# Smaller first loads on two queues, PSUM banks placed by hand, and a root per tile at the end of a transformer block kernel

## The chip, the cores and the metric

The kernel runs on one core of one Trainium2 chip. A time is the device time of one execution in microseconds; a kernel's time is the median of its runs. Engines are named as in the profile: PE (TensorE matmul; PEld its weight loads), DVE (VectorE), ACT (ScalarE), POOL (GpSimd), SP (SyncE, which here only issues DMAs). ACTq, POOLq and SPq rows are DMA issues of those engines.

## The reference

One block over 1024 tokens of width 1024 in fp32, with 16 learned tokens put in front:

```python
h = concat([meta_tokens, x])                       # 1040 x 1024
u = rms_norm(h, pre_mix_norm) @ w_in               # 2560 columns: b, c, h_a, glu_val, glu_gate (512 each)
y_a = b * causal_conv3(c * h_a, conv_a_w)
z   = causal_conv31(glu_val * sigmoid(glu_gate), conv_b_w) + conv_b_bias
y_b = silu(layer_norm(z))
h   = h + rms_norm(concat([y_a, y_b]) @ w_out, post_mix_norm)
n   = rms_norm(h, pre_ffn_norm)
h   = h + rms_norm((silu(n @ w_gate) * (n @ w_up)) @ w_down, post_ffn_norm)   # inner width 2816
return h[16:]
```

## The kernel before

Every fp32 operand is kept as a rounded part (`h`, "hi") and the rest (`l`, "lo"), and `mm3` (L106) makes a product of three matmuls: hi x hi (L108), hi x lo (L109), lo x hi (L110). ACT rounds (a cast), DVE or POOL subtracts to get the rest. The whole program is under a manual schedule: each engine runs its instructions in the order in which the code issues them, and a tile's buffer is taken again when its last reader is done.

**Stage 1, input projection (to about 242 us).** 20 units of 128 output columns: `g`, `v` (gate and value of the long convolution, four each), then `c`, `h`, `b` (four each). A unit is 8 tiles of x (k = 0 to 7) times three thirds of 348 or 342 columns (`T3`, `C3`), or two halves for `b`, so 72 or 48 matmuls. While x arrives, a first pass (L251 to 258) runs the units g0 and v0 side by side over k. Its loads, L199 and L172, are issued on SP: the first 256 columns of g0's weights (`cut[0]`), x tile 0, the same part of v0, then the other 768 columns of each (`cut[1]`) around x tile 1, then the remaining x tiles. `round_x`/`rest_x` (L178, L181) split an x tile, `split_first` (L203, L204) a part of the weights. Ahead of it 12 calls of a warm-up matmul on the identity run on PE (L88; 24 matmuls in the trace). Then 18 one-column matmuls (`ss_x`, L263) sum the squares of x, `spread_x` (L281) turns the nine columns of roots into a row `rB` by transposes, and the 18 other units follow in a loop (L503). `AT` (L501) says at which unit and k extra work is issued: `start_g` (which calls `spread_x`) at unit 0, k = 2. The convolution's taps run on DVE beside the matmuls, `gate` (L294) and `value` read a unit's PSUM.

**PSUM.** Eight banks: in stage 1 a pool `aux` of two and a pool `ps1` of two buffers of three banks. In stages 2 and 3 `aux` stays and `ps2` has six banks; from product 4 of stage 3 on both are closed for a pool `psf` of eight (L942). Buffers of a pool are taken in turn.

**Stage 2, output projection (242 to 339 us).** `group` (L756) runs over three or two blocks of 128 tokens, two banks each, eight k steps, of which the last two go block by block; `at` says what is issued ahead of a step. `leave_psum` evicts, `norms` scales and adds the residual, and `turn` (L590) transposes a normalised block: four transposes into one bank (L595), copied by ACT (L597), twice per block.

**Stage 3, gate and up projection (339 to 768 us).** A Strassen scheme: 11 pairs (`Pair`, index j) of seven products (n = 1 to 7), each product for two weights (m = 0, 1) of 4 x 3 matmuls of 128x512. `order` (L836) interleaves the first two pairs; from then on a pair runs 1, 6, 2, 5, 7, 3, 4. `a_side` forms a weight operand (`op`, L627 on ACT and L614 on DVE) two products ahead; `leave` (L694) evicts one product later: after product 1 a copy on ACT (L698, tile U), after product 2 a Silu and a DVE product (L704, L617, tile G). Products 2 and 4 accumulate on the banks of 1 and 7 once those have been read. `split` (L730) writes hi and lo of a finished tile to DRAM (`gdA`, `gdS`). The loop is at L938.

**Stage 4, down projection (768 us to the end).** Again seven products, 11 steps each, for four banks `QX` or `QY`: `load` (L1022, POOL queue) brings the tiles `a` back four steps ahead, `side` (L1043) splits the weights into `db`, and `leave1` to `leave7` evict. `finish3` scales and stores the first 512 rows, `finish4` (L1154) the rest: for each of the four last tiles an addition, a sum of squares on ACT (L990), a product with the gain, then roots (`rsqrt_n`, L119) for two tiles, one and one, and `scale` (L998) of both halves of a row block with their output DMAs (L1003, SP).

## Time and profile before

| what | value |
| --- | --- |
| time, median of 3 runs | 996.87 us (993.75 to 997.32) |
| the profiled execution | 994.89 us, its span 993.1 us |
| mean granted TensorE clock | 0.995 |
| PE busy | 967.6 us (97%) |
| DVE, ACT, POOL busy | 723.3, 398.4, 279.9 us |
| moved by DMA | 156.68 MB, 158 GB/s over the span |

A row of the timeline gives the start in us from the span's start, the length, engine, line of the code, operation, written tile <- read tiles with partitions x elements, and how many like it were merged; a bracket behind it holds the idle time of the engine before it and what ended that. A row of the waits gives the waiting engine, tile and line, for whom it waited, then the total, the number of times and the longest. Ends of matmuls are modelled, so their rows overlap; starts are what to compare.

### The profile page before, as it was taken

Reading aid. Unit: us, or ns where it says so; the run is one execution under the profiler, and the core shown is the slowest. Engines: PE = TensorE matmul, PEld = TensorE weight load, DVE = VectorE, ACT = ScalarE, POOL = GpSimd, SP = SyncE. Lnnn points to the kernel's source line nnn. Section 1 sums busy time; section 2 is a strip of 40 time slices with the busy share of each in tenths; the row PEclk is TensorE's granted clock in tenths of the full one; section 3 lists DMA queues with packets and bytes.
Section 4 is the critical chain, followed back from the end, with each engine's and each line's share of the span. In section 5 each row is a group of like instructions: output and inputs, shape, how many; then the busy total and the mean of one; then the engine's idle time right before and its main releaser. Section 6 shows DMA issues by size and latency. Waiting matters only on the chain.

```text
span 993.1 us, 12601 instructions
## 1 busy us (share of the span) xinstructions
PE 967.6 (97%) x4643; PEld 829.3 (84%) x4643; DVE 723.3 (73%) x997; ACT 398.4 (40%) x650; POOL 279.9 (28%) x239
## 2 busy tenths in 40 slices
PE   9999999999999989989999999999999999999995
PEld 8999999998878778878888888888887788888784
DVE  6599999556464799998897887887885442545666
ACT  7533322345454663345343433443433333322331
POOL 0367846442000000443133132231242411121110
PEclk9999999999999999999999999999999999999998
DMA  7111211113351520445623624524319899766776
GB/s 281 45 41 44 71 36 43 64 43 148 128 191 64 185 70 0 170 183 199 233 106 128 220 105 142 188 112 166 148 64 340 271 356 370 244 187 201 263 227 230
DMA packets 58285, 156.68 MB, mean 158 GB/s; under 512 B 6128, under 2 KB 6512, under 8 KB 58224
## 3 DMA queue, kind: packets, MB, share of 16 engines
q1 hardware_dynamic: 41904, 104.16, 28.9%
q0 software_dynamic: 11088, 40.38, 12.6%
q10 hardware_dynamic: 5232, 11.35, 3.1%
q8 instruction: 36, 0.59, 0.3%
q14 instruction: 25, 0.20, 0.1%
HBM read 107.10 MB, written 48.76 MB: 157 GB/s over the span
## 4 chain that ended last, share of the span: by engine, by line
PE 85%; DVE 8%; issue 2%; ACT 2%; DMA 1%; ACTq 0%; DVEq 0%; POOL 0%; SPq 0%; POOLq 0%
PE x L108 6%; PE x L109 6%; PE x L110 6%; PE y L108 5%; PE y L109 5%; PE y L110 5%; PE qx L109 4%; PE qx L108 4%; PE qx L110 4%; PE po L108 3%; PE po L110 3%; PE po L109 3%; PE qy L109 3%; PE qy L110 3%; PE qy L108 3%
## 5 line engine op out<-in xcount | busy, mean ns | idle before, releaser
L614 DVE TENSOR_TENSOR op<-u,op 128x512 fp32r<-128x512 f32 x154 | 145.8, 980 | 24.5 <-ACT op L627 23.4
L627 ACT CAST op<-u 128x512 fp32r<-128x512 f32 x154 | 92.0, 619 | 136.1 <-DVE u L614 77.3
L614 DVE TENSOR_TENSOR db<-wb,db 128x512 fp32r<-128x512 f32 x77 | 55.3, 720 | 91.0 <-ACT db L1051 90.7
L617 POOL TENSOR_TENSOR C<-C,C 128x512 f32<-128x512 f32 x11 | 17.6, 1598 | 325.2 <-ACT C L726 175.6
L1051 ACT CAST db<-wb 128x512 fp32r<-128x512 f32 x77 | 47.3, 621 | 122.3 <-PE qx L110 59.4
L108 PE MATMUL qx<-db,a 128*128 128x512 f32 x176 | 68.7, 390 | 2.4 <-DMA a<-gdA 2.4
L109 PE MATMUL qx<-db,a 128*128 128x512 f32 x176 | 68.6, 390 | 0.3 <-DVE db L614 0.3
L110 PE MATMUL qx<-db,a 128*128 128x512 f32 x176 | 68.5, 389 | 0.0
L611 DVE TENSOR_TENSOR U<-y,U 128x512 f32<-128x512 f32 x66 | 43.8, 682 | 23.5 <-PE y L110 23.5
L617 POOL TENSOR_TENSOR U<-U,U 128x512 f32<-128x512 f32 x22 | 31.6, 1437 | 89.3 <-ACT U L726 58.3
L108 PE MATMUL qy<-db,a 128*128 128x512 f32 x132 | 51.5, 390 | 0.6 <-ACT db L1051 0.6
L109 PE MATMUL qy<-db,a 128*128 128x512 f32 x132 | 51.5, 390 | 0.3 <-DVE db L614 0.3
L110 PE MATMUL qy<-db,a 128*128 128x512 f32 x132 | 51.4, 389 | 0.0
L1027 POOL DMA_DIRECT2D a<-gdS x44 | 23.2, 529 | 93.0 <-PE qy L110 47.4
L344 DVE SCALAR_TENSOR_TENSOR ac<-g,pr,ac 128x512 f32<-128x512 f32 x56 | 41.9, 748 | 0.0
L344 DVE SCALAR_TENSOR_TENSOR ae<-d,pr,ae 128x512 f32<-128x512 f32 x56 | 41.9, 748 | 0.0
L108 PEld LDWEIGHTS qx<-db,a 128*128 128x128 f32 x176 | 33.0, 188 | 9.9 <-issue 2.8
L614 DVE TENSOR_TENSOR u<-u,u 128x512 f32<-128x512 f32 x44 | 39.0, 905 | 0.8
L109 PEld LDWEIGHTS qx<-db,a 128*128 128x128 f32 x176 | 33.0, 188 | 7.4 <-DVE db L614 0.6
L108 PE MATMUL x<-B21h,op 128*128 128x512 f32 x88 | 35.1, 399 | 3.9 <-ACT U L698 3.9
L110 PEld LDWEIGHTS qx<-db,a 128*128 128x128 f32 x176 | 33.0, 188 | 6.9
L108 PE MATMUL y<-T2h,op 128*128 128x512 f32 x88 | 34.3, 390 | 1.7 <-DVE G L617 1.7
(303 smaller groups left out, 2924.7 us busy)
## 6 DMA issues: line engine op xcount, KB each, us to landing
a<-gdS POOLq DMA_DIRECT2D x44, 512.0 KB, 4.5
a<-gdA POOLq DMA_DIRECT2D x33, 512.0 KB, 5.6
u<-w_gate_u SPq DMA_DIRECT2D x22, 512.0 KB, 4.5
u<-w_up_u SPq DMA_DIRECT2D x22, 512.0 KB, 5.6
gdS<-HI SPq DMA_DIRECT2D x44, 256.0 KB, 2.3
gdA<-HI SPq DMA_DIRECT2D x33, 256.0 KB, 2.0
gdS<-GS SPq DMA_DIRECT2D x33, 256.0 KB, 2.7
ws_o<-w_out_u SPq DMA_DIRECT2D x14, 512.0 KB, 5.1
```

The source lines that it names most:

```text
L108: nc.tensor.matmul(o, lh, rh, start=start, stop=False, skip_group_check=again)
L109: nc.tensor.matmul(o, lh, rl, start=False, stop=False, skip_group_check=again)
L110: nc.tensor.matmul(o, ll, rh, start=False, stop=stop, skip_group_check=again)
L344: nc.vector.scalar_tensor_tensor(out if i == n - 1 else acc, src[:, i : i + HALF], w(i), init if i == first else acc, op0=ALU.mult, op1=AL ...
L611: (eng or nc.vector).tensor_tensor(o, a, b, op=ALU.add)
L614: (eng or nc.vector).tensor_tensor(o, a, b, op=ALU.subtract)
L617: (eng or nc.vector).tensor_tensor(o, a, b, op=ALU.mult)
L627: nc.scalar.copy(t[:, 0, :], src)
L1027: nc.gpsimd.dma_start(loads[n, j], gd[an][j])
L1051: nc.scalar.copy(t[:, 0, :], b)
```

## The change

- Six calls of the warm-up instead of twelve.
- First loads: x tile 0 in thirds of its columns; weights in parts of 128, 256 and 640 columns (one, two and five k tiles), the first parts of g0 and v0 on ACT's queue, the rest on SP's. The activation table is loaded behind ACT's two issues.
- The first third of the columns of unit g1 (24 of its 72 matmuls) goes into the first pass, into one bank of `aux`; its unit in the loop keeps two thirds. `gate(1)` reads the two places with one more DVE operation.
- The transposes of `spread_x` are issued in three places (unit 0, k = 2, 4, 6), in the bank of `ss_x`.
- From stage 2 on there are eight pools of one bank. The output projection's blocks take the banks (2, 7), (3, 4), (5, 6), the turns (0, 1), (5, 6) or (2, 7), and the products a list `free`: each takes the first two and gives them back after its eviction.
- Turns are issued one step earlier and one at a time; at product 2 of the order, product 1 is evicted before the turns and not behind them; at product 15 the eviction comes before the splits.
- The first three loads of `a` for stage 4 are issued at the last product of stage 3.
- In stage 4 the product with the gain is issued behind the additions of the same step; at the end each tile has a root of its own, with that product inside it, and its two halves are scaled apart, the second in the wait of the next tile.

The diff, cut:

```diff
-    for i in range(12):
+    for i in range(6):
         nc.tensor.matmul(pw[:, :P], ident, ident, start=True, stop=True)
...
-    def rsqrt_n(ss, inv_n, e, n, name):
+    def rsqrt_n(ss, inv_n, e, n, name, middle=None):
...
         nc.vector.tensor_scalar(v, ss, inv_n, e, op0=ALU.mult, op1=ALU.add)
+        if middle:
+            middle()
...
-    cut = [slice(0, 2 * P), slice(2 * P, D)]
+    cut = [slice(0, P), slice(P, 3 * P), slice(3 * P, D)]
+    FIRST = [("g", 0), ("v", 0), ("g", 1)]
...
-    for j in range(2):
-        load_first("g", cut[j])
-        xs[j] = load_x(j)
-        load_first("v", cut[j])
-    for k in range(2, 5):
+    xs[0] = load_x(0, [third(0)])
+    load_first(FIRST[0], cut[0], nc.scalar)
+    load_first(FIRST[1], cut[0], nc.scalar)
+    table(AF.Abs_reciprocal_sqrt)
+    load_first(FIRST[2], cut[0])
+    for j in (1, 2):
+        nc.sync.dma_start(xs[0][:, third(j)], xT[0][:, third(j)])
+    xs[1] = load_x(1)
+    for u in FIRST:
+        load_first(u, cut[1])
+    xs[2] = load_x(2)
+    for u in FIRST:
+        load_first(u, cut[2])
+    for k in range(3, 5):
         xs[k] = load_x(k)
...
+    split_first(FIRST[0], cut[0])
+    round_x(0, third(0))
+    rest_x(0, third(0))
+    for u in FIRST[1:]:
+        split_first(u, cut[0])
+    for j in (1, 2):
+        round_x(0, third(j))
+        rest_x(0, third(j))
     round_x(1)
     rest_x(1)
-    split_first("v", cut[1])
+    for u in FIRST:
+        split_first(u, cut[1])
...
     for k in range(2, KD):
         round_x(k)
+        rest_x(k)
+        if k == 2:
+            for u in FIRST:
+                split_first(u, cut[2])
         square_x(k - 2)
-        rest_x(k)
...
+    for j in range(3):
+        for u in FIRST[: 3 if j == 0 else 2]:
+            mm_first(u, 0, (j,))
+    for k in range(1, KD - 2):
+        for u in FIRST:
+            mm_first(u, k)
+    for u in (FIRST[0], FIRST[2], FIRST[1]):
+        for k in range(KD - 2, KD):
+            mm_first(u, k)
...
-    AT = {(0, 2): start_g, (14, 1): ln_mean, (15, 3): ln_var, (15, 7): ln_spread}
+    AT = {(0, 2): lambda: spread_x(NT, NT + 1), (0, 4): lambda: spread_x(0, 4), (0, 6): start_g, (14, 1): ln_mean, (15, 3): ln_var, (15, 7): ln_spread}
...
-    ps2 = pa.enter_context(tc.tile_pool(name="ps2", bufs=6, space=PSUM, reuse_waits="tile"))
+    banks = [ctx.enter_context(tc.tile_pool(name=f"b{i}", bufs=1, space=PSUM, reuse_waits="tile")) for i in range(8)]
+    OUT_BANKS = [(2, 7), (3, 4), (5, 6)]
+    free = [5, 6, 3, 4, 0, 1, 2, 7]
...
-            return lambda: [self.leave(n, m, self.pb[where, m]) for m in range(2)]
+            def left():
+                for m in range(2):
+                    self.leave(n, m, self.pb[where, m])
+                    if n not in (1, 7):
+                        free.append(self.at[where, m])
+            return left
...
-    s1, left = group((3, 4, 5), middle, {1: ahead(0, 5), 2: ahead(1, 6), 3: ahead(2, 7), 4: turns(0, 1), 5: turns(2)})
+    s1, left = group((3, 4, 5), middle, {1: ahead(0, 5), 2: ahead(1, 6), 3: lambda: [ahead(2, 7)(), turns(0)()], 4: turns(1), 5: turns(2)})
...
-        turns(3, 4, 5)()
+        turns(4, 5, at=(5, 6))()
...
-    s1, left = group((6, 7), up, {1: ahead(5), 2: lambda: [split_o(6), pairs[0].load(0)], 3: pairs_load, 6: early})
+    s1, left = group((6, 7), up, {1: ahead(5), 2: lambda: [split_o(6), pairs[0].load(0)], 3: pairs_load, 5: turns(3), 6: early})
...
-        if s == 4:
-            pa.close()
-            psf = ctx.enter_context(tc.tile_pool(name="psf", bufs=8, space=PSUM, reuse_waits="tile"))
         done = pairs[j].product(n, made.pop(s))
         if s == 2:
-            turns(6, 7)()
+            results.pop(1)()
+            turns(6, 7, at=(2, 7))()
...
-        if s in (14, 15):
+        if s == 14:
             pairs[first_splits[s][0]].split(*first_splits[s][1:])
-        results.pop(s - 1)()
+        if s == len(order) - 1:
+            for q in range(3):
+                load(1, "A11", q, "ws")
+        results.pop(s - 1, lambda: None)()
+        if s == 15:
+            pairs[first_splits[s][0]].split(*first_splits[s][1:])
...
-                for f in todo[:k]:
-                    f()
+                for g in [f() for f in todo[:k]]:
+                    if g:
+                        g()
...
         squares(4 + i, 0, t)
-        mul(t, t, g0)
+        return lambda: mul(t, t, g0)
...
-        leave4(0, QX[0])
-        for f in rest[1:]:
-            f()
-        leave4(1, QX[1])
-        r = root(0, 2)
-        rows(4)
-        leave4(2, QX[2])
-        r.update(root(2, 3))
-        leave4(3, QX[3])
-        rows(5)
-        r.update(root(3, 4))
-        rows(7)
-        rows(6)
+        meanwhile = rest[1:]
+        for i in range(4):
+            times = leave4(i, QX[i])
+            for f in meanwhile:
+                f()
+            r = root(i, times)
+            one, two = left(i)
+            one()
+            meanwhile = [two]
+        two()
```

More of the change, by code (lines that the diff above doesn't have):

```diff
@@ L588, in norms, with turn @@
         return n
-    def turn(i, n):
+    def turn(i, n, at=(0, 1)):
         c = slice((i % 4) * P, (i % 4 + 1) * P)
         for q in range(2):
-            pt = aux.tile([P, 512], F32, tag="a", name=f"pt{i}_{q}")
+            pt = bank(at[q], f"pt{i}_{q}")
             for k in range(4):
@@ L756, in group @@
     def group(grp, ks, at):
-        pm = {i: [ps2.tile([P, 512], F32, tag="p", name=f"po{i}{q}") for q in range(2)] for i in grp}
+        pm = {i: [bank(b, f"po{i}{q}") for q, b in enumerate(OUT_BANKS[j])] for j, i in enumerate(grp)}
         def mm(i, k):
@@ L936, in hybrid_block, with load @@
     later_splits = {6: ("A22", "S3", "S1"), 2: ("A11", "S2"), 5: ("A12",), 7: ("S4",)}
-    psf = None
+    loads = {}
+    def load(n, an, j, tag):
+        if (n, j) not in loads:
+            loads[n, j] = wp.tile([P, 2, 512], F32R, tag=tag, name=f"a{n}_{j}")
+            nc.gpsimd.dma_start(loads[n, j], gd[an][j])
     for s, (j, n) in enumerate(order):
@@ L981, in keep @@
         return hold[n]
-    QX = [bank(f"qx{i}") for i in range(4)]
-    QY = [bank(f"qy{i}") for i in range(4)]
+    free += [i for i in range(8) if i not in free]
+    QX = [bank(free[i], f"qx{i}") for i in range(4)]
+    QY = [bank(free[4 + i], f"qy{i}") for i in range(4)]
     ssq = [[sm.tile([P, 16], F32, tag="sp", name=f"sp{t}{dh}", bufs=4) for dh in range(2)] for t in range(2)]
@@ L1007, in use_b @@
             wd[j][b] = WB[b, g][:, j % 4, :]
-    work, loads, made = [], {}, {}
+    work, made = [], {}
     later_b = {3: (1, 2), 12: (2, 0), 14: (2, 1), 16: (2, 2), 19: (3, 0), 21: (3, 1), 23: (3, 2)}
@@ L1020, in hybrid_block, with load_step @@
     AHEAD = 4
-    def load(s):
+    def load_step(s):
         if s < len(work):
             n, j, an = work[s][:3]
-            tag = "wl" if n == 4 and j >= 9 else ("ws", "wh")[s // 3 % 2]
-            loads[n, j] = wp.tile([P, 2, 512], F32R, tag=tag, name=f"a{n}_{j}")
-            nc.gpsimd.dma_start(loads[n, j], gd[an][j])
+            load(n, an, j, "wl" if n == 4 and j >= 9 else ("ws", "wh")[s // 3 % 2])
     ready = {}
@@ L1134, in one @@
         def one(ti):
-            scale(ti, r[:, ti : ti + 1], (hold["D11"][:, ti, :], hold["E1"][:, ti, :]))
+            for q, t in enumerate(("D11", "E1")):
+                scale(ti, r[:, ti : ti + 1], hold[t][:, ti, :], q)
             residual(4 + ti)
@@ L1151, in leave4, with root, left @@
         squares(4 + i, 0, t)
-        mul(t, t, g0)
+        return lambda: mul(t, t, g0)
     def finish4(rest):
-        def root(a, b):
-            c = slice(a, b)
-            tot = sm.tile([P, 16], F32, tag="tot", name=f"tot{a + 1}")
-            add(tot[:, : b - a], ssq[1][0][:, c], ssq[1][1][:, c])
-            r = rsqrt_n(tot[:, : b - a], 1.0 / D, RMS_EPS, b - a, f"out{4 + a}")
-            return {4 + i: r[:, i - a : i - a + 1] for i in range(a, b)}
-        def rows(ti):
-            scale(ti, r[ti], (hold["E5"][:, ti - 4, :], hold["D22"][:, ti - 4, :]))
+        def root(i, middle):
+            tot = sm.tile([P, 16], F32, tag="tot", name=f"tot{i + 1}")
+            add(tot[:, :1], ssq[1][0][:, i : i + 1], ssq[1][1][:, i : i + 1])
+            return rsqrt_n(tot[:, :1], 1.0 / D, RMS_EPS, 1, f"out{4 + i}", middle)
+        def left(i):
+            return lambda: scale(4 + i, r, hold["E5"][:, i, :], 0), lambda: scale(4 + i, r, hold["D22"][:, i, :], 1)
         for f in rest[:1]:
             f()
-        leave4(0, QX[0])
-        for f in rest[1:]:
-            f()
-        leave4(1, QX[1])
-        r = root(0, 2)
-        rows(4)
-        leave4(2, QX[2])
-        r.update(root(2, 3))
-        leave4(3, QX[3])
-        rows(5)
-        r.update(root(3, 4))
-        rows(7)
-        rows(6)
+        meanwhile = rest[1:]
[8 more added lines that the diff above has]
+        two()
     down(1, "A11", lambda j: wd[j][0], QX, True, leave1)
@@ L1188, in hybrid_block @@
     for q in range(AHEAD):
-        load(q)
+        load_step(q)
     wd = [[None] * 4 for j in range(NP)]
```

115 lines of the change are left out of this document (55 added, 60 removed).

## The prediction

> **What bounds the kernel now.** I read the page first, then the waits of TensorE, then the timeline and the busy time by stage around each of those waits.
>
> ```profile
> span 993.1 us, 12601 instructions
> PE 967.6 (97%) x4643; PEld 829.3 (84%) x4643; DVE 723.3 (73%) x997; ACT 398.4 (40%) x650; POOL 279.9 (28%) x239
> ```
>
> TensorE is busy for 967.6 of 993.1 us. The change removes only six of its calls, so its whole reach is the 25.5 us in which TensorE does nothing, and slow clock. Where they lie (waiting engine, for whom; total, times, longest):
>
> ```profile
> PE x L108 <- ACT U L698: 3.9, 2, 2.7
> PE pt L595 <- ACT raw L597: 2.9, 4, 1.2
> PE qx L108 <- DMA a<-gdA: 2.4, 1, 2.4
> PE y L108 <- DVE G L617: 1.7, 1, 1.7
> ...
> PE po L108 <- DVE cv L405: 0.7, 1, 0.7
> PE qy L108 <- ACT db L1051: 0.6, 1, 0.6
> PE qy L109 <- DVE db L614: 0.3, 1, 0.3
> ```
>
> The rest is the start and the tail. Each has an edit, so I take them in order of time.
>
> **1. Start: gain 1.8.** Timeline rows (start, length, engine, line, out<-in, idle before):
>
> ```profile
> 0.75 0.41 ACTq L133 DMA_DIRECT2D pr<-par  x1
> 1.19 1.28 ACT L117 ACT_TABLE_LOAD   x1 [1.19 <-PEq L1244]
> 1.37 5.49 PE L88 MATMUL warm<-ident 128*128 128x128 f32 x24 [1.37 <-POOL xh L213]
> 3.15 0.40 ACT L203 CAST wh_g<-ws_g 128x256 fp32r<-128x256 f32 x1 [0.47 <-DMA ws_g<-w_in_u]
> 5.23 1.16 ACT L178 ACTIVATE xh<-xs,pr 128x1040 fp32r<-128x1040 f32 x1 [1.67 <-DMA xs<-xT]
> 6.42 1.30 DVE L181 SCALAR_TENSOR_TENSOR xl<-xs,pr,xh 128x1040 fp32r<-128x1040 f32 x1 [2.41 <-ACT xh L178]
> 7.87 0.40 PE L109 MATMUL p_g<-xl,wh_g 128*128 128x348 f32 x1 [0.71 <-DVE xl L181]
> ```
>
> The second real matmul starts at 7.87, because the whole x tile must land (5.23), be rounded (1.16) and have its rest formed (1.30). After: two weight loads go on ACT behind the parameters, at 0.41 each, so the table load runs from about 2.1 to 3.4 and its dummy to 3.6. The data of the first third is there by then (the 128 KB first part, issued at 0.75, was cast at 3.15). Then a cast of 128 columns (0.3, below the 0.40 of 256), a third of the 1.16 (0.45) and a third of the 1.30 (0.5): second matmul at 4.8, 3.1 earlier. Six calls of warm-up fewer end at about 4, ahead of that.
>
> The gain is not 3.1, because of the clock. The 24 warm passes take 5.49/24 = 0.23 us each, while transposes of the same width (in 3) take under 0.13: the array begins at about half rate.
>
> ```profile
> 7.90:30.60 22.70, 22.70 (x142) 22.45 (x143) 20.04 (x18) 18.16 (x18) 0.00 (x0) 1.00 0.56 215
> 434.30:437.60 3.30, 2.96 (x7) 2.38 (x8) 3.30 (x3) 1.82 (x4) 3.22 (x3) 0.50 0.98 378
> ```
>
> (Busy time by stage: length, PE (count), PEld, DVE, ACT, POOL, granted clock, DMA share, GB/s.) From 7.9 on a 348-wide matmul comes every 22.7/142 = 0.16, so the clock has risen by then, after the warm passes ended at 6.9; I take 7.5. If it rises at the same moment after the change, the 2.7 us from 4.8 give 9 matmuls and not 17, so 1.3 is lost: 1.8 remains. If it misses that moment, as TensorE pauses between 4 and 4.8, a slow stretch like that of the last row (3.3 us, half the matmuls) costs 1.6 more and leaves 0.2: that is rival C. The Trainium skill, "TensorE: Matmul & The Clock Gate", section "What's actually happening", says that half rate is the default and that full rate follows a busy window of about 3.4 us; the two rows agree with it, and by it the shorter warm-up speaks against this edit.
>
> Will x and weights keep up? Per k the pass now has 7 x 3 = 21 matmuls, 3.4 us. The first DMA stretch moves 383 GB/s:
>
> ```profile
> 3.00:13.00 10.00, 9.29 (x51) 8.70 (x50) 5.96 (x7) 6.70 (x9) 0.78 (x3) 1.00 0.98 383
> ```
>
> Up to the end of x1 there are 0.08 + 0.53 + 0.20 + 0.53 = 1.34 MB (parameters, x0, three first parts, x1), 3.5 us at that rate; counted from 2.7 it lands near 6.2, and with 1.16 and 1.30 its rest is ready at 8.6, while k = 0 keeps TensorE until about 9.2. Up to x3 there are 2.43 MB more: 12.5, rest by 15.2; TensorE needs it at 9.2 + 6.7 = 15.9. So no new stall, by under 1 us. The moved third (24 matmuls, 3.8 us) is the same work elsewhere: no cost. The three-step spread comes at k = 2, 4, 6 of a shorter unit, some 2.4 us later, and the gate has one more DVE operation (0.5); VectorE's conv chain starts that much later. This row hides it, VectorE waiting 10 us for TensorE behind that chain; without the cover it would cost 3:
>
> ```profile
> 193.21 1.23 DVE L392 TENSOR_TENSOR cs<-p_h,cs 128x1026 f32<-128x1026 f32 x1 [10.21 <-PE p_h L110]
> ```
>
> Bounds: -1.0 (clock a window late, x1 late by 1) to +3.1 (all of it).
>
> **2. Banks at the output projection: 0.7.** The first group waits 0.7 at `po` for VectorE to read the last unit's PSUM. The first two banks by hand are 2 and 7, which the last `b` unit does not fill. Bounds 0 to 0.8.
>
> **3. The first two places of turns: 2.7.** There a `turn` waits until ScalarE has emptied one of two banks. By stage, then one row of the timeline:
>
> ```profile
> 292.16:295.26 3.10, 1.88 (x18) 1.64 (x16) 0.69 (x1) 1.72 (x4) 0.00 (x0) 1.00 1.01 400
> 328.93:333.41 4.48, 3.02 (x25) 2.48 (x24) 1.39 (x2) 2.84 (x6) 0.00 (x0) 1.00 0.95 350
> 355.28:358.86 3.58, 2.18 (x17) 1.63 (x15) 3.51 (x7) 2.69 (x6) 0.00 (x0) 1.00 0.41 122
> ```
>
> ```profile
> 292.16 1.03 PE L595 MATMUL pt<-ident,hn 128*128 128x128 f32 x8
> ```
>
> Eight transposes take at most 1.03 when nothing holds them, so 16 need 2.06 of the 3.10 and 24 need 3.1 of the 4.48: 1.0 + 1.4, and 0.3 more because the 1.03 holds the drain of the last. After, one row block is turned per step, some 3 to 4 us apart, and the fourth and fifth have other banks. Their copies (0.5 each on ScalarE) lie beside matmuls. Bounds 1.5 to 3.1.
>
> **4. The first products: 4.9, less than the waits there.** The third stretch above has 16 transposes in 3.58 (1.5 too many, part of it the U copy, which is now ahead of the turns); the wait for G costs 1.7; the wait for U 2.7 and a slow stretch behind it, in which 7 matmuls (row 434.30 above, clock 0.50) take what 14 take: 1.5. Together 7.4. But VectorE sits under it (rows of three engines in order of time, those between left out):
>
> ```profile
> 377.55 0.69 DVE L611 TENSOR_TENSOR U<-y,U 128x512 f32<-128x512 f32 x1 [1.84 <-PE y L110]
> 434.01 1.07 ACT L698 COPY U<-x 128x512 f32<-128x512 f32 x2
> 434.64 0.79 PE L108 MATMUL x<-B21h,op 128*128 128x512 f32 x1 [2.73 <-ACT U L698]
> 436.67 3.47 DVE L614 TENSOR_TENSOR op<-u,op 128x512 fp32r<-128x512 f32 x2
> 441.61 0.39 PE L108 MATMUL y<-T1h,op 128*128 128x512 f32 x1
> ```
>
> After 377.55 VectorE no longer waits for TensorE until past 446; what idles it there is ScalarE, for 0.6 at most. So its chain can move up by 1.84 and no more. The operand of product (2,5) is ready half way through the 3.47, at 438.4, and used by the third matmul of that product, 0.46 after 441.61: slack 3.6. TensorE can gain 1.84 + 3.6 = 5.4 there, not 7.4; then it waits for VectorE. The two U copies, which now come ahead of the splits' casts, delay those by 1.07, half of which I charge: 4.9. Bounds 1.8 (only the VectorE part) to 7.4.
>
> **5. Loads ahead of the down projection: 2.4.**
>
> ```profile
> 758.17 1.29 POOL L617 TENSOR_TENSOR C<-C,C 128x512 f32<-128x512 f32 x1 [18.70 <-DVE C L611]
> 765.16 3.38 POOL L1027 DMA_DIRECT2D a<-gdA  x6
> ```
>
> Three loads move from 765.2, behind GpSimd's next product, to 759.5, behind this one; the first landed 5.3 after its issue (770.5, where TensorE's wait ended) and would land by 765, before the last product's end at 768.2. GpSimd is held 3 x 0.56 = 1.7 longer, and its next product starts at 763.6 anyway: no cost; without that gap 1.7 on the sums. Next late is the operand of step 3, about 1 us early. Bounds 0 to 2.4.
>
> **6. Evictions of the down projection: 1.6.** VectorE row:
>
> ```profile
> 931.40 0.69 DVE L617 TENSOR_TENSOR D<-D,gB_out 128x512 f32<-128x512 f32 x1 [0.79 <-ACT jo L990]
> ```
>
> Each eviction is add, square on ScalarE, product, and VectorE idles 0.79 for the square; four in a row made the operand late (waits of 0.6 and 0.3 at `qy`, 0.3 at `qx`, each with a restart of 0.1). Two adds first and the products behind them save 1.4 per pair, more than the lateness. Bounds 0 to 2.
>
> **7. Tail: 2.9.** VectorE, ScalarE, SyncE:
>
> ```profile
> 982.61 0.69 DVE L611 TENSOR_TENSOR E<-qx,E 128x512 f32<-128x512 f32 x1 [0.28 <-PE qx L110]
> 984.09 0.69 DVE L617 TENSOR_TENSOR E<-E,gB_out 128x512 f32<-128x512 f32 x1 [0.79 <-ACT jo L990]
> 986.02 0.15 DVE L611 TENSOR_TENSOR tot<-sp,sp 128x1 f32<-128x1 f32 x1
> 987.10 0.75 DVE L1002 SCALAR_TENSOR_TENSOR E<-E,r_out,hr 128x512 f32<-128x512 f32 x1
> 989.09 0.74 DVE L1002 SCALAR_TENSOR_TENSOR D<-D,r_out,hr 128x512 f32<-128x512 f32 x1
> 989.86 0.33 SPq L1003 DMA_DIRECT2D out<-D  x1
> ```
>
> Now: add and square until 984.09, product, two scalings of another tile, the root (986.02 to 987.10), four scalings of 0.66. After: the sum at 984.09, product inside the root (which takes 1.5 then), first half at 985.6, second at 986.2, last issue at 987.0 and not 989.9. The tile before is done with the same chain before this bank is, so it doesn't push. Bounds 2 to 2.9.
>
> **Sum.** 1.8 + 0.7 + 2.7 + 4.9 + 2.4 + 1.6 + 2.9 = 17.0. The profiled execution took 994.89, so 977.9; I say 978. The median of the runs, 996.87, is 2.0 above that execution; they spread over 3.6.
>
> **Rivals.** A (the forecast), 978.
>
> B, VectorE takes all of the wait at 431 back: the middle gives 1.8 and the time is 981. For it: the 3.47 for two operands, beside GpSimd's sums, which a longer delay by the U copies would push. Against: 3.6 of slack.
>
> C, the clock at the start rises a stretch later, or parts of x come late: 980; with B 983.
>
> D, the banks by hand don't release earlier, and the waits of 2, 3 and G stay: 0.7 + 2.7 + 1.7 less, 983. Against: their releasers (copies, G) belong to other tiles than the ones wanted next.
>
> E, the other side: a bank that is taken from the list is not yet empty. There are 77 products; a wait of w at each costs 77w, so from w = 0.22 the gain is gone and from 0.29 the kernel is slower by over 5; at 0.4 it is 1009. For it: the list is in order of eviction, which VectorE and ScalarE set, and VectorE's share is 73%. Against: products hold at most four to six of eight banks, and the waits above show no product that waits for a bank after 437.
>
> F, several of these together, up to within 5 us: 991.
>
> **Numbers.** A 0.60, B 0.15, C 0.12, D 0.05, F 0.04, E 0.04. About 0.5% (5 us) is what a measurement can tell here: A to D are faster (0.92), F the same, E slower. Range: below, 978 less the rest of the upper bounds of 1, 4 and 6 (1.3 + 2.5 + 0.4), and 2 to 3 for the spread: 971; above, B and C together plus the 2.0 to the median and some of D: 987.
>
> **What would show it.** The sums of squares start here now:
>
> ```profile
> 30.88 1.97 PE L263 MATMUL ss_x<-ones,sa 128*128 128x1 f32 x18
> ```
>
> Right: second real matmul before 5, full pitch from about 7.5, `ss_x` starting near 33, which is 1.8 ahead of this row plus the moved 3.8; no wait of TensorE for `raw`, for G or for a load of `a`; the clock at 1.00 around 430, with a wait of about 1 for VectorE's `op` in its place; the last output issued 4.5 and not 7.3 after the last bank. Wrong: half pitch beyond 8 us, waits of products for VectorE or ScalarE that recur per pair, or a wait for `op` at 431 to 450 above 3.

## The result and the profile after

The changed kernel takes 987.12 us (median of 6 runs, 985.37 to 990.15), the kernel before 994.96 (6 runs, 991.76 to 997.32): ratio 0.993, 95% interval 0.9913 to 0.9947. The forecast was 978, with 971 to 987 for its range. The profiled execution took 985.37; its sum in the forecast was 977.9, so 7.5 us are missing; the median, 987.12, is another 1.8 us longer and lies just outside the range. The page after, first the span and TensorE's busy time:

```profile
span 983.6 us, 12612 instructions
PE 964.9 (98%) x4631; PEld 827.4 (84%) x4631; DVE 723.8 (74%) x1007; ACT 397.9 (40%) x657; POOL 280.5 (29%) x239
```

The view of TensorE's waits after (waiting engine, line, for whom: total, times, longest):

```profile
PE qx L108 <- DMA a<-gdA: 2.3, 1, 2.3
PE y L109 <- DVE T2l L647: 1.8, 1, 1.8
PE y L110 <- DVE op L647: 1.6, 1, 1.6
PE warm L88 <- POOL xh L229: 1.4, 1, 1.4
PE qx L108 <- ACT db L1099: 1.3, 1, 1.3
PE x L108 <- ACT U L739: 1.0, 1, 1.0
PE po L108 <- DVE cv L433: 0.7, 1, 0.7
```

Against the list of before: the waits for `raw` (2.9 us), for G (1.7) and for `db` at `qy` (0.6 and 0.3) are gone, U has fallen from 3.9 to 1.0, `cv` stands as it was. New are T2l, `op`, `db` at `qx`; the wait for `a` has the same name as before but is another one, at 960 us and not at 768. Following one and the same matmul through both traces shows where the time went. Lead is its start before less its start after; c2 is a kernel of the experiments below.

| matmul | before | after | lead | c2 |
| --- | --- | --- | --- | --- |
| first of the output projection (`po`) | 242.16 | 242.70 | -0.5 | 242.96 |
| first of the gate and up projection (`x`) | 338.95 | 336.13 | 2.8 | 336.40 |
| first of the down projection (`qx`) | 770.56 | 762.14 | 8.4 | 759.15 |
| end of the span | 993.1 | 983.6 | 9.5 | 977.6 |

Between the rows of this table: the lead was 4.75 just ahead of product 4, 2.7 behind the wait for T2l, 7.7 at the product that used to wait for U, 5.9 behind the wait for `op`, 6.6 behind the wait for `db` at 770 us, 8.8 at 960 us and 6.3 behind the wait for `a` there. So part of what was won was taken back at four places. Each has its rows.

VectorE and TensorE at 360 us, timeline (start, length; idle before in the bracket):

```profile
356.83 1.29 DVE L647 TENSOR_TENSOR T2r<-raw,raw 128x512 f32<-128x512 f32 x2
359.33 1.29 DVE L647 TENSOR_TENSOR op<-u,op 128x512 fp32r<-128x512 f32 x2 [1.21 <-ACT op L660]
360.54 1.29 DVE L647 TENSOR_TENSOR T2l<-T2r,T2h 128x512 fp32r<-128x512 f32 x2
361.88 0.50 PE L109 MATMUL y<-T2l,op 128*128 128x512 f32 x1 [1.84 <-DVE T2l L647]
```

TensorE's second matmul of product 4 reads T2l. On VectorE that stands behind the two differences for `op`, and those first waited 1.21 us for ScalarE. All this was so in the kernel before (there with the same 1.21 us), but TensorE came later. T2r there, to set beside 356.83:

```profile
358.73 1.28 DVE L614 TENSOR_TENSOR T2r<-raw,raw 128x512 f32<-128x512 f32 x2
```

VectorE's lead here is 1.9 us, while TensorE's just ahead of product 4 is 4.75. Then VectorE at 431 us, after and, in the second block, before:

```profile
430.24 1.78 DVE L647 TENSOR_TENSOR C<-C,HI 128x512 fp32r<-128x512 f32 x1
431.94 3.46 DVE L647 TENSOR_TENSOR GS<-GS,HI 128x512 fp32r<-128x512 f32 x2
435.33 1.28 DVE L647 TENSOR_TENSOR op<-u,op 128x512 fp32r<-128x512 f32 x2
```

```profile
432.70 0.68 DVE L614 TENSOR_TENSOR C<-C,HI 128x512 fp32r<-128x512 f32 x1
433.31 3.44 DVE L614 TENSOR_TENSOR GS<-GS,HI 128x512 fp32r<-128x512 f32 x2
```

Three differences of a split stand ahead of the operand that TensorE waits for until 436.06. They did so before as well, ahead of the row of 436.67 in the prediction; VectorE's order there is the same in both kernels. They now take 5.1 us, each 1.7 instead of 0.69, and took 4.0 before: VectorE's slow operations are those that run beside GpSimd's four sums, and the first of these now starts at 428.01 and not at 432.81.

Then ScalarE and TensorE at 770 us:

```profile
755.32 0.53 ACTq L1024 DMA_DIRECT2D gB_out<-g_out  x1
770.12 1.06 ACT L1124 ACTIVATE gB_out<-gB_out 128x1024 f32<-128x1024 f32 x1 [3.61 <-DMA gB_out<-g_out]
771.74 0.50 PE L108 MATMUL qx<-db,a 128*128 128x512 f32 x1 [1.28 <-ACT db L1099]
```

ScalarE holds `db` of step 3 back for the multiply of the output gain, whose load took 14.8 us from issue to landing (8.0 in the kernel before, where the three early `a` loads were not ahead of it; 7.9 in f1 of the experiments, the changed kernel without them). The wait of 1.3 us is the mildest of the ten traces that have both this load order and this multiply: in the other nine TensorE waits 1.8 to 3.9 us here. Last, GpSimd's and SyncE's issues and TensorE at 960 us, and the busy time of the stretch (granted clock, DMA share and GB/s in the last three columns):

```profile
954.53 0.34 SPq L1053 DMA_DIRECT2D out<-D  x1
955.05 0.53 POOL L983 DMA_DIRECT2D a<-gdA  x1 [1.67 <-PE qx L110]
955.63 0.43 SPq L1047 DMA_DIRECT2D hr<-hd  x1
963.17 0.47 PE L108 MATMUL qx<-db,a 128*128 128x512 f32 x1 [2.30 <-DMA a<-gdA]
```

```profile
955.00:960.00 5.00, 5.00 (x23) 4.14 (x23) 4.02 (x7) 0.00 (x0) 0.53 (x1) 1.00 1.05 346
```

The last `a` load, issued at 955.05, landed at 963.04, 8.0 us later; before it took 3.6 (963.08 to 966.66). The output rows and residual loads (`hr`) began 2.1 us behind its issue then, and 0.5 us ahead of it now, because the evictions ahead of them got shorter.

### The profile page after: what moved, and what is told of

It reads as the page before. It is cut to its first block, busy times and chain, and to the rows that moved or that the text cites. A ratio compares the mean times of both kernels' runs of the same rounds, so it can differ in the third digit from the quotient of the medians.

```text
span 983.6 us, 12612 instructions
## 1 busy us (share of the span) xinstructions
PE 964.9 (98%) x4631; PEld 827.4 (84%) x4631; DVE 723.8 (74%) x1007; ACT 397.9 (40%) x657; POOL 280.5 (29%) x239
## 5 line engine op out<-in xcount | busy, mean ns | idle before, releaser
L109 PE MATMUL y<-T2l,op 128*128 128x512 f32 x88 | 34.4, 391 | 1.8 <-DVE T2l L647 1.8
L110 PE MATMUL y<-T1h,op 128*128 128x512 f32 x88 | 34.4, 390 | 1.6 <-DVE op L647 1.6
```

What stands on the lines that cost most here:

```text
L109: nc.tensor.matmul(o, lh, rl, start=False, stop=False, skip_group_check=again)
L110: nc.tensor.matmul(o, ll, rh, start=False, stop=stop, skip_group_check=again)
```

## Experiments

Single traces are compared with the changed kernel's profile at the same matmul. A run without an interval (e1 to e8, b2) is one execution, and those of the changed kernel spread over 8.5 us (a2), so it is read by its waits and not by its time. Each ratio is against runs of the kernel before on the same chip.

**1. The gain's multiply later (e1).**

```diff
+            if s == 6:
+                nc.scalar.mul(gO, gO, RSCALE)
             if s == 1:
                 last()
                 table(AF.Abs_reciprocal_sqrt)
-                nc.scalar.mul(gO, gO, RSCALE)
```

> The changed kernel with one edit: the output gain is multiplied by its constant at step 6 of the down projection instead of step 1; the three early loads of a stay. Theory (ScalarE's queue): the multiply waits 3.61 us for the load of the gain, and db of step 3 stands behind it in the same queue; so TensorE's wait for ScalarE's db (1.28 us) and for VectorE's db after it (0.2 us) at 770 us both go, and the lead over the kernel before stays near 8.4 us across the seam instead of falling to 6.6. Rival (bandwidth): the early loads take bandwidth from the operands of the first products of the down projection themselves; then a wait of about 1 to 2 us for a DMA, wb or a, stands in the place of the wait for db, and the lead still falls to about 6.6.

The wait for `db` is gone and none came in its place: at that seam the kernel gained 1.9 us on the changed one. The theory holds. But at 960 us the load of `a` was awaited 3.89 us and not 2.30, and then the clock fell (TensorE's row, then the busy time behind it):

```profile
962.00 0.77 PE L108 MATMUL qx<-db,a 128*128 128x512 f32 x1 [3.89 <-DMA a<-gdA]
```

```profile
962.00:965.00 3.00, 3.00 (x7) 2.42 (x8) 1.34 (x3) 0.61 (x2) 0.00 (x0) 0.50 0.94 375
```

Seven matmuls in 3 us at a clock of 0.50: some 2 us more were lost there, and the run took 986.49.

**2. The last residual rows behind the last `a` load (e2).**

```diff
-        (nc.scalar if ti < 4 else nc.sync).dma_start(hr[ti], hd[ti])
+        (nc.scalar if ti < 4 else nc.gpsimd).dma_start(hr[ti], hd[ti])
...
             load_step(s + AHEAD)
+            if s + AHEAD == len(work) - 1:
+                residual(4)
+                residual(5)
...
-            residual(4 + ti)
+            if ti > 1:
+                residual(4 + ti)
```

> The changed kernel with one edit: the loads of the last four residual rows (hr, 512 KB each) go to the queue of the a loads, behind the last a load, instead of SyncE's queue ahead of it. Theory (the hr loads and the early output rows share the DMA engines with the last a load): the a load lands 4 to 5 us after its issue at 955 instead of 8.0, and TensorE's wait of 2.3 us at 960 falls under 0.5 us. Rival (the a loads' own queue is the limit: three of them issued within 2.7 us): landing still takes 7 us or more and the wait stays over 1.5 us. Between the two: the output rows alone, which still start at 954.5, keep 1 us of it. The last rows could wait for hr in the tail instead: then the tail is longer by what the wait shows.

The load landed 5.8 us after its issue, and TensorE did not wait; 984.78 us. That lies between the two predictions (4 to 5, 7 or more). It speaks for the theory, but see experiment 6.

**3. T2l ahead of the operand's differences (e3).**

```diff
-            a_side(4)
             for i in range(2, 4):
                 t2_lo(i)
+            a_side(4)
```

> The changed kernel with one edit: in the third product's step, VectorE's second half of T2l comes before the two differences of the left operands of product 4 instead of behind them. Theory (VectorE's order): T2l ends 1.2 us earlier, at about 360.6 instead of 361.8, and TensorE's wait for it (1.8 us) falls to about 0.6 us, and the lead after it is 3.9 us instead of 2.7. Rival 1 (the turns' copies on ScalarE set it): T2l starts when T2h is ready, 358.1 and 358.8, and the wait goes to zero, with a wait for op of under 0.6 us in its place. Rival 2 (the lead is only lent): what is won here is taken back at the next wait on VectorE, since VectorE has no idle time until 370.

Rival 1 is right. VectorE no longer idles between T2r and `op`, TensorE waits for neither, and nothing of it was lost at the next waits on VectorE but 0.5 us at U:

```profile
357.30 1.29 DVE L647 TENSOR_TENSOR T2l<-T2r,T2h 128x512 fp32r<-128x512 f32 x2
358.51 1.29 DVE L647 TENSOR_TENSOR op<-u,op 128x512 fp32r<-128x512 f32 x2
```

(In the eleven traces with the changed kernel's order the wait for T2l was 0.9 to 1.9 us, in eight of them 0.9 to 1.1; 1.0 us is its usual price.)

**4. The split behind the operand (e4).**

```diff
-        if s == 15:
-            pairs[first_splits[s][0]].split(*first_splits[s][1:])
...
         a_side(s + LEAD)
-        if s in first_splits and s not in (14, 15):
+        if s in first_splits and s != 14:
             pairs[first_splits[s][0]].split(*first_splits[s][1:])
```

> The changed kernel with one edit: the split of A22, S2 and S4 of the first pair, 5.2 us of VectorE in the profile because GpSimd's sums run beside it, stands behind the operands of product 17 instead of ahead of them. Theory (the order on VectorE makes the wait): op of product 17 is ready by 433.5 instead of 436, TensorE's wait of 1.6 us for it goes, and the lead stays near 7.7 us instead of falling to 5.9. Rival (the eviction behind it): the split now delays the evictions U<-y and the operands of product 18 by its 5 us; a wait of 1 to 2 us appears at product 18 or 19 and the lead falls to 6 all the same.

The wait of 1.6 us is gone, and 0.3 us of it came back until 442 us: the theory holds for the wait, the rival does not. The run took 989.76 all the same, since it waited 2.4 us for `db` at 770 us and 3.8 for `a` at 960, each with a half-speed stretch behind it. The same two waits had been 1.3 and 2.3 us in the changed kernel's profile.

**5. The third row tile in other banks (e5).**

```diff
     OUT_BANKS = [(2, 7), (3, 4), (5, 6)]
+    FIRST_BANKS = [(2, 7), (3, 4), (0, 1)]
...
```

> The changed kernel with one edit: the third row tile of the first group of the output projection takes banks 0 and 1 instead of 5 and 6. Theory (which bank): banks 5 and 6 are the two that after_b(3) still reads, 0 and 1 have been free since the gains of the normalisation, so TensorE's wait of 0.7 us for VectorE's cv goes and the lead at the first products of the gate and up matrices is 3.5 instead of 2.8 us. Rival 1: the operands are as late as the bank (VectorE's yl of the last part), and the same 0.7 us appears as a wait for yl. Rival 2: the turns of row tile 0, which use banks 0 and 1 in the next group, now wait for the eviction of this row tile: a wait of pt of up to 1 us.

Neither theory: the wait of 0.7 us stayed. Its row names the place, the fourth matmul of the group, which is the first on bank 7:

```profile
244.74 0.50 PE L108 MATMUL po<-wh_o,yh 128*128 128x512 f32 x1 [0.69 <-DVE cv L433]
```

Bank 7 holds nothing of the last `b` unit, but belongs to its tile of three banks, and the tile is given back as a whole.

**6. All five edits (c1) and the changed kernel again (a2)**, now with banks (2, 0), (3, 4), (1, 7) in the first group.

> The changed kernel with five edits together: the gain's multiply at step 6, the last residual rows behind the last a load, T2l ahead of the operands of product 4, the split behind the operands of product 17, and banks (2,0), (3,4), (1,7) for the first group of the output projection (in the trace with the third row tile moved, the wait of 0.7 us stood at the fourth matmul, the first on bank 7, which shares one three-bank tile with the two that VectorE still reads). Theory (five separate waits, each paid once): 1.5 + 2.3 + 1.8 + 1.6 + 0.7 = 7.9 us of waits in the changed kernel's profile go, 977 to 980 us, the forecast of the whole change, and the runs lie closer together, since the half-speed stretches of 2 us behind the waits at 770 and 960 us go too. Rival (a lead is taken back at the next late operand, as at each place in the changed kernel): 982 to 985 us, with new waits of 1 us or more behind at least two of the five.

> The changed kernel once more, with a second trace. Theory (its waits at 770 and 960 us differ from run to run, since they are what the load of the gain and the last a load take): 985 to 991 us again, and in this trace the wait for db of 1 to 4 us and the wait for a of 1.5 to 4.5 us, with matmuls at half pitch for 2 us behind any that is near 2 us or longer. Rival (the first trace is typical): both waits within 0.3 us of 1.3 and 2.3, no half-speed stretch.

c1: 982.75 us (981.65 to 983.26), ratio to before 0.9871, interval 0.9855 to 0.9888. a2: 989.12 us (984.88 to 993.39), ratio 0.9936, interval 0.9911 to 0.9961; in its trace `db` was awaited 2.5 us and `a` 1.8, both without a half-speed stretch. So the five edits take 6.4 us off and nearly all of the spread, and c1 is some 4 us short of the theory. The waits of c1:

```profile
PE qx L108 <- DMA a<-gdA: 2.5, 1, 2.5
PE warm L88 <- POOL xh L229: 1.4, 1, 1.4
PE x L108 <- ACT U L740: 1.2, 1, 1.2
PE po L108 <- DVE jk L594: 0.9, 1, 0.9
PE qx L108 <- ACT db L1098: 0.6, 1, 0.6
PE po L109 <- DVE w_o L169: 0.6, 1, 0.6
```

The wait for `cv` is gone, but first a wait for the weights `w_o` took its time back (256 us), and then the second group waited for bank 7, which now is emptied last in the first (`jk`, 278 us): against the changed kernel the bank edit cost 1.2 us. And the load of `a` was late again, 8.2 us from issue to landing with the residual rows behind it as in e2 (5.8 us). That order alone is not what decides.

**7. The last two `a` loads issued earlier (f2), the early loads undone (f1).** First f2, in `load_step`, then f1:

```diff
+    last_a = []
...
+            if n == 4 and j >= 9:
+                if j == 9:
+                    last_a.append(blocks(big("a4_9", F32R)))
+                loads[n, j] = last_a[0][:, 2 * j - 18 : 2 * j - 16, :]
+                nc.gpsimd.dma_start(loads[n, j], gd[an][j])
+                return
```

```diff
-        if s == len(order) - 1:
-            for q in range(3):
-                load(1, "A11", q, "ws")
```

> The changed kernel with one edit: the last two a loads go to a buffer that has been free for long, so they are issued behind the one before them at 950 to 951 us instead of 952.9 and 955.1, ahead of the output rows at 954.5. Theory (time of issue: the load meets the rows' traffic only because it starts with it): both land by 957, TensorE's wait for a at 960 us (1.6 to 4.4 us in the traces) is gone in every run, and the median falls by 2 to 4 us to 983 to 986, the half-speed stretch behind the wait included. Rival (the queue of a loads is itself behind: each lands in turn 3 us after the other): the last still lands past 959 and a wait of over 0.5 us stays.

> The changed kernel with one step undone: the three a loads issued ahead of the last product go back behind the product's evictions, as in the kernel before. Theory (the wait only changed its name): the wait for db at 770 us goes and one of 2 to 4 us for a comes back at the first product of the down projection; 986 to 989 us, no difference to the changed kernel that the interval can tell. Rival 1 (the step is worth its 2.4 us): 989 to 992 us. Rival 2 (the step costs, since the load of the gain took 8.0 us before and 14.8 after): 984 to 986 us.

f2: 985.70 us (984.75 to 987.93), ratio 0.9916, interval 0.9899 to 0.9933. The last load was issued 7.3 us ahead of the time at which TensorE could use it, not 5.7; it still took 7.8 us, and the wait was 0.5 us. The theory had the load landing by 957 us and the wait gone; it landed at 963.5, so the rival is right that the load itself is no faster: it only has to be issued earlier. The median lies in the theory's range, but the intervals of f2 and of the changed kernel overlap. f1: 986.05 us (984.41 to 989.66), ratio 0.9923, interval 0.9903 to 0.9943: no difference to the changed kernel. In its trace TensorE waits 2.3 us for `a` at 763 us and not for `db`. The early loads, forecast at 2.4 us, are worth nothing that these runs can tell.

**8. Four places mended (c2):** the edits of e1 to e4 and of f2 together, the banks as in the changed kernel.

> The changed kernel with the gain's multiply at step 6, T2l ahead of the operands of product 4, the split behind the operands of product 17, the last residual rows behind the last a load, and the last two a loads issued early; the banks of the output projection as in the changed kernel. Theory (with the bank edit out, 1.2 us, and the wait for a at 960 us gone, 2.5 us, against 982.75 us of the five together): 978.5 to 980 us, which is what was forecast for the change itself. Rival (the tail then waits for the residual rows or the evictions): 981 to 983 us with a new wait behind 960 us.

c2: 978.68 us (978.01 to 979.48), ratio 0.9839, interval 0.9821 to 0.9857. That is the number forecast for the change without these edits, but not by its terms (see below). The wait for `a` at 957 us, which the theory had gone, is still 1.1 us. All its waits:

```profile
PE x L108 <- ACT U L739: 1.5, 1, 1.5
PE warm L88 <- POOL xh L229: 1.4, 1, 1.4
PE qx L108 <- DMA a<-gdA: 1.1, 1, 1.1
PE po L108 <- DVE cv L433: 0.7, 1, 0.7
PE p_g L108 <- ACT xh L183: 0.6, 1, 0.6
PE p_c L110 <- POOL wl_c L154: 0.2, 1, 0.2
```

**9. The start: twelve warm-up matmuls (e6), x0 in one transfer (e7), the old start in the new kernel (e8), the new start in the old kernel (e9), the kernel before again (b2).** The edits of e6 and e7:

```diff
-    for i in range(6):
+    for i in range(12):
         nc.tensor.matmul(pw[:, :P], ident, ident, start=True, stop=True)
```

```diff
-    xs[0] = load_x(0, [third(0)])
+    xs[0] = load_x(0)
...
-    for j in (1, 2):
-        nc.sync.dma_start(xs[0][:, third(j)], xT[0][:, third(j)])
```

> The changed kernel with one edit: 12 warm-up matmuls again instead of 6. Theory A (the clock): the clock rose at 7.57 us with twelve and at 9.42 us with six, because the array was busy from earlier on; with twelve it rises near 7.6 us again, the matmuls from 5.9 to 9.2 us run at 0.15 us each instead of 0.29, but they then wait for x1's remainder at 11.23 us as before, so nothing is won: the lead at the normalisation (194 us) stays -0.5 us, within 0.2. Theory B (the clock was what the start lost): the lead there rises by 1 us or more. If the twelve themselves hold TensorE past 5.5 us, the second real matmul starts that much later.

> The changed kernel with one edit: x0 is loaded by one transfer of 4 KB rows instead of three of 1.4 KB; the weights keep their small parts. Theory (small rows move slowly): the transfers run at 211 and 284 GB/s up to 8.7 us with the small parts and ran at 329 and 394 before; with x0 in one piece the rate is over 300 and x1 lands at 8.0 us or earlier instead of 8.65; the start is then 0.3 to 0.6 us better. Rival (the order of the bytes decides, not their size): x1 lands at 8.5 to 8.7 as now, and the first real matmuls start 1 to 1.5 us later, since the whole of x0 lands near 6.5 us, while TensorE's start of the second pass moves by less than 0.2 us.

> The changed kernel with the whole start of the kernel before: its cuts and order of first loads, twelve warm-up matmuls, no third of the second gate unit, three extra banks for the spreading. Theory (the new start costs): the lead at the normalisation rises from -0.54 to 0 and stays so to the end, 0.5 us less in all. Rival (the new start gives what was forecast, 1.8 us, and something behind it takes it back before 194 us): then without it the wait for POOL's wl_c at 103 us and the turns of the gate stay, and the lead falls below -0.5, to -1 or -2.

> The kernel before with the new start alone: small first parts on two queues, six warm-up matmuls, a third of the second gate unit in the first pass, the spreading in three places. Theory (the first passes end when x1 lands, 26.0 us ahead of the end in every trace with the new start, and x1 lands when it did): no difference, within 0.1%, and the normalisation's matmuls at 194.5 to 195.4 us. Rival 1 (the forecast): 1.8 us faster. Rival 2 (the old start can lose its clock: in the trace with the start undone the clock rose at 11.3 us and the normalisation came at 195.80, in that of before at 7.6 us and 194.32): faster by 0.5 to 1 us in the median, since the new start never loses it.

> The kernel before once more, for a second trace. Theory (its start has two courses): the normalisation's first matmul at 194.3 or near 195.8 us, by whether the clock rises at 7.6 or 11.3 us. Theory (its wait for a at 769 us, 2.4 us in the first trace, varies with the landing of six loads issued together): 2 to 4 us. Rival: both as in the first trace within 0.2 us.

e9 gives the answer: 994.64 us (12 runs, 992.08 to 997.66), ratio to before 0.9993, interval 0.9979 to 1.0006. That is 0.5 us in the median, and no difference that the runs can tell; the forecast 1.8 (0.9982) lies at the edge of the interval, so it takes the traces to rule it out. The normalisation's first matmul came at 194.4 to 195.4 us in all traces with the new start, and at 194.32, 194.74 and 195.80 (before, b2, e8) with the old: none of the new is ahead of the first of these. (b2 lies between the two courses that it expected, and waits 2.1 us for `a` at 770 us.) e8 expected a lead of 0 instead of -0.5 and showed -1.5. There the old start lost its clock, which costs most of that (ten matmuls in this stretch, seventeen in the trace of before; busy time by stage, clock third from the end):

```profile
8.70:11.30 2.60, 2.60 (x10) 2.60 (x10) 1.76 (x2) 2.01 (x3) 0.00 (x0) 0.50 1.03 419
```

e6: theory A, the clock is up from 5.7 us and TensorE then waits 0.6 us for x1's rest; 0.25 us behind the changed kernel at 194 us. e7: half of the theory. The transfers moved 361 and 354 GB/s in the two stretches of its expectation, and x1 landed at 6.7 us and not at 8.65; but its rest was begun only at 9.47 us, with six warm-up calls TensorE idled 1.7 us ahead of x0, its clock was 0.50 until 11.3 us, and the sums of squares came at 35.11, 0.45 later than in the changed kernel.

**10. Both at once (c3):** c2 with x0 whole and twelve warm-up matmuls.

> The four edits of c2 and, in the start, x0 in one transfer and twelve warm-up matmuls. Theory (x1's landing and the clock set the end of the first pass): x1 lands near 7 us instead of 8.0 to 9.2, the clock is up by 8 us because TensorE is not idle from 4 to 6 us, and the matmuls of the sums of squares (ss_x) start at 33.0 to 33.6 us instead of 34.2 to 35.4, so 977 to 978 us in all, 1.2 us under c2. Rival (the small weight parts, now landing at 7 to 8 us, or ScalarE's and VectorE's work on a whole x0 are as late): ss_x at 34.2 us or later and the time as c2, 978.0 to 979.5.

c3: 978.65 us (978.40 to 979.23), ratio 0.9848, interval 0.9832 to 0.9865, as c2: the rival. In order, of the changed kernel and of c3, the first matmul that needs the rest of x1, and the sums of squares:

```profile
11.23 0.43 PE L109 MATMUL p_g<-xl,wh_g 128*128 128x348 f32 x1 [0.33 <-DVE xl L186]
...
34.66 0.94 PE L291 MATMUL ss_x<-ones,sa 128*128 128x1 f32 x8
```

```profile
11.46 0.43 PE L109 MATMUL p_g<-xl,wh_g 128*128 128x348 f32 x1
...
34.89 0.72 PE L289 MATMUL ss_x<-ones,sa 128*128 128x1 f32 x6
```

The distance is 23.43 us in both (and 23.47 in e6): from the rest of x1 on, TensorE works without a pause. In c3 the first part of v0 landed at 7.54 us instead of 5.76, and all that ScalarE does behind it, x1 included, moved with it, so that x1's landing at 7.4 us gained nothing. With all variants of the new start the sums of squares came at 34.2 to 35.2 us.

## Why the prediction was wrong, step by step

The direction was right. Of the seven terms three came as forecast or better (turns, evictions, tail) and four were too large: the start by 2.3 us, the banks by 0.7, the first products by 1.8, the early loads by 1.8. A cost of 2.5 us was not in the sum.

- **1. Start, forecast 1.8, measured -0.5 in this profile and 0 in the runs** (e9). The second real matmul came at 5.50 us (forecast 4.8), but that was not what bounds the pass. The failed step is the question whether x and weights keep up: it took 383 GB/s from the kernel before and had x1's rest ready at 8.6 us. It was ready at 11.2, since x1 landed at 8.65 us and not at 6.2. The count was too short for the kernel it came from: by it the 1.8 MB up to the end of x1 there land at 7.4 us, and they landed at 8.36. Stretches of the changed kernel, and then of the kernel before:

```profile
3.00:5.60 2.60, 2.01 (x9) 1.42 (x7) 0.87 (x2) 1.42 (x4) 0.59 (x3) 1.00 0.84 211
5.60:8.70 3.10, 3.10 (x11) 2.93 (x12) 1.66 (x4) 1.59 (x5) 0.00 (x0) 1.00 1.00 284
```

```profile
3.00:5.60 2.60, 2.60 (x15) 2.60 (x14) 0.43 (x1) 0.78 (x2) 0.78 (x3) 1.00 0.92 329
5.60:8.70 3.10, 2.39 (x12) 2.05 (x12) 2.28 (x3) 2.23 (x4) 0.00 (x0) 1.00 1.01 394
```

  The DMA engines were about as busy (shares of 0.84 and 1.00 for 0.92 and 1.01), but moved 211 and 284 GB/s with the small parts instead of 329 and 394. The first of these is steady: 211 to 252 in all traces with x0 in thirds, 289 to 329 with the old start, 354 and 361 with x0 whole (c3, e7). The second is not (258 to 373 with the thirds). x1 landed at 8.0 to 9.2 us with the thirds and at 8.4 to 8.9 with the old start: the new start brought it in no earlier, and with x0 in thirds the sums of squares come 26.0 to 26.2 us behind that landing in all thirteen traces, that of e6 with its earlier clock included. Of rival C it is the second half, parts of x late, that came; the clock did rise later too (full pitch from 9.46 us, one of the prediction's signs of being wrong), which cost nothing, as e6 shows.
- **2. Banks at the output projection, forecast 0.7, measured 0.** Bank 7 was taken for free, but it is given back with the two that are read (e5); and with banks that are free the weights are as late (c1). This is rival D's first 0.7; its other waits went.
- **3. Turns, forecast 2.7, measured 3.4** (lead from -0.5 to 2.8). Right.
- **4. First products, forecast 4.9, measured 3.1** (2.8 to 5.9). The old waits went, but for 1.0 us at U, and the half-speed stretch too. The cap by VectorE is the mis-sized term. Both its parts were right: VectorE's chain moved up by 1.9 us at 377 us, and the operand had its slack of 3.6. But they were added to TensorE's lead, 2.8 us at the first product, and VectorE's own lead was 1.9 there (358.73 against 356.83; it had just waited 1.7 us for ScalarE's `op` between 332 and 336, 0.3 in the kernel before). Then 0.3 us went at a wait for ScalarE's `op` at 384, and 1.1 at the split, which ran more of its time beside GpSimd's sums: 1.9 + 1.9 - 0.3 - 1.1 + 3.6 = 6.0, TensorE's lead at that product. That TensorE, with the larger lead, would also run into T2l at 360 us was not seen (e3: 1.0 to 1.8 us). The split can stand behind the operand instead, which takes the 1.6 us away (e4). This is rival B in part.
- **5. Loads ahead of the down projection, forecast 2.4, measured 0.6 in the profile and nothing in the runs** (f1). The wait for `a` went. "Next late is the operand of step 3, about 1 us early" named the right operand, and left out that its cast stands behind a multiply (e1) that waits for a load which the moved loads slow down (f1: 7.9 us without them, 14.8 with them).
- **6. Evictions, forecast 1.6, measured 2.1.** Right. Its consequence was missing: the rows of the first half are finished 10.7 us earlier, their traffic meets the last `a` load, and 2.5 us are lost at 960 us (f2, c2). This is the cost that no rival had.
- **7. Tail, forecast 2.9, measured 3.2.** The last bank's addition, its product inside the root, the last scaling and the last output's issue, 4.7 us after the last matmul at 975.99:

```profile
976.41 0.69 DVE L644 TENSOR_TENSOR E<-qx,E 128x512 f32<-128x512 f32 x1 [0.48 <-PE qx L110]
978.16 0.68 DVE L650 TENSOR_TENSOR E<-E,gB_out 128x512 f32<-128x512 f32 x1
979.92 0.75 DVE L1052 SCALAR_TENSOR_TENSOR D<-D,r_out,hr 128x512 f32<-128x512 f32 x1
980.70 0.33 SPq L1053 DMA_DIRECT2D out<-D  x1
```

In sum: -0.5 + 0 + 3.4 + 3.1 + 0.6 + 2.1 - 2.5 + 3.2 = 9.4, the 9.5 us by which the span is shorter. Rival E did not happen: no product waits for a bank from the list. What happened is parts of B, C and D together, and the cost of step 6 on top.

That c2 takes 978.7 us is therefore no late confirmation of the sum. Its lead is -0.8 us at the output projection (start and banks were to give 2.5), 2.6 at the first product, so 3.4 from the turns (2.7), 11.4 at the down projection, so 8.8 from the first products and the early loads (7.3), and 15.5 at the end, so 4.1 from evictions and tail (4.5). Start and banks stay 3.3 us short; the turns make up 0.7 of that and the products 1.5, these with the edits of e3 and e4, which the forecast did not have.

What stays open: what exactly the `a` load at 960 us shares. In that stretch the DMA engines are at a share of 1.05, and issuing the load earlier helps, while putting the `hr` loads behind it in its own queue helped once (e2) and not the next time (c1); with both edits it still took 8.5 us (c2). The Trainium skill, "DMA: Bandwidth & Descriptors", section "Issuing engines are not separate DMA queues", says that transfers of all issuing engines end up on the same 16 DMA engines and interleave, whoever issued them. The trace of f1 agrees: the gain's load on ScalarE's queue took 7.9 us once the three `a` loads on GpSimd's queue were no longer ahead of it, and 14.8 with them. That the load at 960 us (8.0 us for 3.6) was slowed by the rows on SyncE's queue is likely, but no run shows it by itself.

## What to carry to other kernels

When a wait is removed, follow the lead to the next operand on every engine, and to every transfer that will now start earlier: here the gain was taxed by three operands that stood behind something which nobody needed yet, on VectorE or ScalarE, and by one load that met traffic which now came sooner, and mending these four places was worth as much again (987.1 to 978.7 us). A cap by another engine is counted from that engine's own lead, not from that of the engine whose wait is removed: VectorE's was 1.9 us where TensorE's was 2.8. A multiply that waits for a load does not belong ahead of operands in an in-order queue, however small it is. A transfer rate read from a trace holds for the sizes in that trace: with x0 in thirds the transfers from 3.0 to 5.6 us moved 211 to 252 GB/s, and the tile that mattered, x1, landed no earlier than in the kernel before; with x0 whole they moved 354 to 361, and x1 landed at 6.7 and 7.4 us.

## What the runs showed of the hardware

A short pause of TensorE can cost more than itself. Counting the pauses without any TensorE work behind 240 us in all traces: all six of 3.5 us and over (3.6 to 4.6) were followed by matmuls at 0.43 us each instead of 0.23, for 7 to 12 of them, 1.4 to 2.4 us lost; of the 18 between 2.0 and 3.0 us nine were and nine were not; of those under 2.0 us one was (1.9). e2 and e3 stand for the two sides, 2.9 us without and 1.9 us with such a stretch. The Trainium skill, "TensorE: Matmul & The Clock Gate", section "What's actually happening", has a free-running window of about 3.4 us and says that the clock falls after an idle window; the long pauses agree, but half of the pauses shorter than that window brought the fall as well; the shortest was 1.9 us.

Where a pause lies counts, and not only how long it is. In all eighteen traces the granted clock changes on a grid: between the first change and the last, every stretch at 1.00 lasted a whole multiple of 3.41 us, and every one at 0.50 lasted 3.41 us or twice that. Laid on the grid of its own trace, the pauses sort better than by length. Of the fourteen with 2.0 us or more of idle time within one cell, thirteen were followed by the fall; of all the others, up to 2.7 us long, three were, all at `db` (770 us), where shorter pauses follow at once. The nine of eighteen are thus for the most part a matter of where the pause fell, which no edit here sets. That the fall depends on the idle time in a cell is a reading of these counts; no run varied it by itself.

The spread of the changed kernel (985 to 993 us) is of the size of its two waits at 770 and 960 us with and without such stretches, and it shrank to 978.0 to 979.5 in c2, where the first is gone and the second 1.1 us.
